# Making a triangular inverse by block rows in the chunk preparation of a gated DeltaNet layer

## The chip, the cores and the metric

The kernel runs on one core of a Trainium2 chip. A core has five engines with queues of their own: TensorE (PE in the profile, with its weight loads as PEld), VectorE (DVE), ScalarE (ACT), GpSimd (POOL) and SyncE (SP), which here only issues DMAs. Each engine works through its queue in order. Matrix products land in PSUM, and DVE or ACT bring them into SBUF. The metric is the device time of one execution in microseconds (us), as the median of several runs.

## The reference

One layer of a diffusion backbone: a gated DeltaNet scan (group A, 4 heads of 128), neighbourhood attention (group B), an output projection and a feed-forward part. Only the preparation of group A matters here. Per chunk of tokens, head and scan direction, the reference solves with a unit triangular matrix:

```python
m = jnp.where(strict, jnp.einsum("bhncd,bhnmd->bhncm", kb, k) * decay, 0.0)
a_mat = jnp.eye(CHUNK, dtype=f32) + m
u = lax.linalg.triangular_solve(a_mat, v * beta[..., None], left_side=True, lower=True, unit_diagonal=True)
w = lax.linalg.triangular_solve(a_mat, kb * jnp.exp(gam)[..., None], left_side=True, lower=True, unit_diagonal=True)
...
v_new = u_i - jnp.einsum("bhck,bhkv->bhcv", w_i, S)
```

There are 1024 latent and 256 context tokens, scanned forward and backward from the context's final state.

## The kernel before

The kernel works on 1280 tokens, features by tokens, in stages: modulation and norm (up to about 60 us), the input projection in blocks of 128 columns (to about 610 us), then the scan beside the attention (to about 850 us), the output projection, and the feed-forward part. Chunks of the scan are 128 tokens here, so there are 10 chunks (2 of context) in each of 2 directions, 20 in all, and each has 4 heads.

The input projection runs over a list of jobs. A `Block` job makes 128 columns with 8 steps of 9 (or 6) matrix products (line 389, tile `blk`); a `Wide` job makes 256 or 264 columns for one token tile after the other (line 572). Both use weights and activations split into a high and a low float32r part, so three products stand for one. Between these products the loop at lines 1008 to 1015 (and 994 to 1007) calls `bg.step(n)`, which moves a background generator on by `n` yields. One of these is `preps()` (line 853), which prepares the chunks.

`preps()` keeps up to three `prep` generators alive and gives each one step in turn, so three chunks are interleaved. It starts after `block_inverses()`, which has inverted all 32x32 diagonal blocks and stored them and their transposes in `x_d`. The first four chunks are those of the context; the others start only when the queries' blocks are done. Within one `prep`:

- Two products with the decay mask (`rg`, line 886, on POOL) are prepared. The diagonal blocks are copied from the loaded tile `xc` into zeroed tiles: the transposed ones into `fx` (ACT, line 891), the inverses into `x0` (POOL, line 892).
- Lines 896 and 897 make the decay exponents in PSUM; line 900 takes the exponential into `e` (ACT). Line 902 multiplies the key products `kk` by it, one DVE instruction per head. The diagonal 32x32 blocks of `kk` are zero, and it is strictly triangular in blocks.
- Line 910 multiplies `kk` by the diagonal inverses (4 heads, one product each), and ACT copies the result over `kk`, now called `f` (line 912).
- Three rounds follow (lines 916 to 922). Each makes `f`-transposed times the present estimate for all 4 heads, 128x128 each (line 919), and DVE adds `x0` into `y` (line 920). With four blocks on the diagonal, the third round is exact.
- `y` is stored in `y_d` (line 929, on SP) two steps later, and the scan reads it from there (line 1067).

Tile `y` is the same buffer as `e` (tag `y`, 4 buffers); `x0` has 3 buffers and `fx` 2, all zeroed once by POOL at line 866. A product of float32 operands appears in the trace as two passes, each a weight load (PEld) and a matrix product (PE). The order of instructions on each engine is fixed when the program is built.

Of the kernel before, what the change touches and what calls it, by code (L numbers as in the profile page):

```python
# [14 lines left out]
OP = mybir.AluOpType  # L15
# [72 lines left out]
def hybrid(ctx, tc, a, dbg):  # L88
    nc = tc.nc
    pe, act, dve, pool, sp = nc.tensor, nc.scalar, nc.vector, nc.gpsimd, nc.sync  # L90

    def pools(stack, name, side=None, bufs=1, **kw):
        if side:
            kw["side"] = side
        return stack.enter_context(tc.tile_pool(name=name, bufs=bufs, reuse_waits="tile", **kw))

    def shift(stack, name, side, n):

        pools(stack, name, side).tile([128, n], F32, name=name, tag=name)
# [142 lines left out]
    hs = [slice(h * 128, h * 128 + 128) for h in range(4)]  # L242
# [117 lines left out]
    with ExitStack() as bs:  # L360
# [7 lines left out]
        def bank(name="m"):  # L368

            if len(psum) == 1:  # L370
                return psum[0].tile([128, 512], F32, name=name, tag="ps")
            return psum[1].tile([128, 512], F32, name=name, tag=name, bufs=4 if name == "blk" else 2)
# [229 lines left out]
        with ExitStack() as xs:  # L602
# [67 lines left out]
            for s0, n in SEGS:  # L670
                p = bank()
# [7 lines left out]
            for k in range(KT):  # L679
# [3 lines left out]
                t = xt[k]  # L683
# [165 lines left out]
        fl = lambda x: x.rearrange("p a b -> p (a b)")  # L849
# [3 lines left out]
        def preps():  # L853

            first_half.close()
            with ExitStack() as gs:
                pk = pools(gs, "pk", "left")
                shift(gs, "ppad", "left", 64)
                pp = pools(gs, "pp", "left")

                def work(name, bufs=2, dt=F32):
                    return (pk if name == "kk" else pp).tile([128, 4, 128], dt, name=name, tag=name, bufs=bufs)

                x0s, fxs = [[work(f"{m}{i}", 1) for i in range(k)] for m, k in (("x0", 3), ("fx", 2))]
                for t in x0s + fxs:
                    pool.memset(t, 0.0)

                def fetch(d, c):

                    kk, xc = work("kk", 4), pp.tile([128, 2, 4, 32], F32, name="xc", tag="xc", bufs=3)  # L870
                    sp.dma_start(kk, kk_d[:, c])
                    sp.dma_start(xc, x_d[:, d, :, c * 4:c * 4 + 4])
                    at = None
                    if c >= 2:
                        at = work("at", 3)
                        sp.dma_start(at, qk_d[:, c - 2])
                    return d, c, kk, xc, at

                def prep(n, d, c, kk, xc, at):
                    lat = c >= 2  # L880
                    mle = M[C_LE + d].rearrange("p (o i) -> p o i", o=1).to_broadcast([128, 4, 128])
                    rgs = []
                    for gg in (GH, GL):
                        rg = work("rg", 2, F32R)
                        src = gg.bitcast(F32)[:, d, c].rearrange("p (h o) -> p h o", o=1).to_broadcast([128, 4, 128])
                        pool.tensor_tensor(rg, src, mle, OP.mult)
                        rgs.append(rg)
                    x0, fx = x0s[n % 3], fxs[n % 2]
                    for b in range(4):
                        q = slice(b * 32, b * 32 + 32)  # L890
                        act.copy(fx[q, :, q], xc[q, 1])
                        pool.tensor_copy(x0[q, :, q], xc[q, 0])
                    yield 1
                    p = bank("pr")
                    for j, rg in enumerate(rgs):
                        pe.matmul(p, mr[:, d], fl(rg), start=j == 0, stop=False)
                    pe.matmul(p, mr[:, 4], mneg[:, d].rearrange("p (o i) -> p o i", o=1).to_broadcast([128, 4, 128]),
                              start=False, stop=True)
                    e = work("y", 4)
                    act.activation(fl(e), p, AF.Exp)  # L900
                    for h in range(4):
                        dve.scalar_tensor_tensor(kk[:, h], kk[:, h], NB[:, d, c, h:h + 1], e[:, h],
                                                 op0=OP.mult, op1=OP.mult)
                    if lat:
                        dve.tensor_tensor(at, at, e, OP.mult)
                        stores.append((at_d[d, c - 2], at, tick[0] + 2))
                    yield 1
                    p = bank("pr")
                    for h in range(4):
                        pe.matmul(p[:, hs[h]], kk[:, h], fx[:, h], start=True, stop=True)  # L910
                    f = kk
                    act.copy(fl(f), p)
                    yield 1
                    y = e
                    src = x0
                    for _ in range(3):
                        p = bank("pr")
                        for h in range(4):
                            pe.matmul(p[:, hs[h]], f[:, h], src[:, h], start=True, stop=True)  # L919
                        dve.tensor_tensor(fl(y), p, fl(x0), OP.add)  # L920
                        src = y
                        yield 1
                    stores.append((y_d[d, c], y, tick[0] + 2))

                stores, tick = [], [0]

                def flush(n):
                    while stores and stores[0][2] <= n:
                        sp.dma_start(*stores.pop(0)[:2])

                todo = [(d, ORDER[d][i]) for i in range(NCH) for d in range(2)]
                live, landing = [], []
                n = 0
                while live or todo or landing:
                    if not landing and todo and (todo[0][1] < 2 or all(x in done for x in queries)):
                        landing.append(fetch(*todo.pop(0)))
                    if landing and len(live) < 3:
                        live.append(prep(n, *landing.pop(0)))
                        n += 1
                    if not live:  # L940
                        yield
                    nxt = []
                    for g in live:
                        tick[0] += 1
                        flush(tick[0])
                        if next(g, 0):
                            nxt.append(g)
                        yield
                    live = nxt
                flush(tick[0] + 2)  # L950
# [23 lines left out]
        for n in range(2, len(jobs) + 2):  # L974
            j = jobs[n] if n < len(jobs) else None
            if n == inv:
                bg2.drain()
                bg2s.close()
                early.close()
                psum.append(bs.enter_context(tc.tile_pool(name="psa", bufs=1, space=PSUM)))  # L980
                bg.add(block_inverses())
                bg.add(preps())
# [52 lines left out]
    fl = lambda x: x.rearrange("p a b -> p (a b)")  # L1035
# [185 lines left out]
    class Stream:  # L1221
# [67 lines left out]
        def next(self, n=2):  # L1289

            while len(self.got) < n:
                self.make()
            out = [self.got.pop(0) for _ in range(n)]
            return out
# [21 lines left out]
    with ExitStack() as os_:  # L1316
# [3 lines left out]
        for k in range(4):  # L1320
            raw = wp.tile([128, KT, 132], F32, name="wraw", tag="wraw", bufs=2)[:, :, :128]
            sp.dma_start(raw, na_d[k].rearrange("p (i t) -> p i t", t=128))
            n = nap.tile([128, 2, L], F32R, name=f"na{k}", tag=f"na{k}")
# [18 lines left out]
        for b in range(KT - 2):  # L1342
# [3 lines left out]
            for k in range(KT):  # L1346
                for j, (wi, xi) in enumerate(((0, 0), (0, 1), (1, 0))):
                    for o, s in zip(outs, HV):
                        pe.matmul(o, w[wi][:, k], parts[xi][k][:, s], start=k == 0 and j == 0,  # L1349
                                  stop=k == KT - 1 and j == 2)  # L1350
# [14 lines left out]
        for t, s in enumerate(HV):  # L1365
            outs = [bank(), bank()]
            last.append(outs)
            for k in range(KT):
                for j, (wi, xi) in enumerate(((0, 0), (0, 1), (1, 0))):
                    for o, w in zip(outs, ws):  # L1370
                        pe.matmul(o, w[wi][:, k], parts[xi][k][:, s], start=k == 0 and j == 0,  # L1371
                                  stop=k == KT - 1 and j == 2)
# [9 lines left out]
    with ExitStack() as us:  # L1382
        xc = pools(ctx, "xc", "right")
# [172 lines left out]
    for n, (wn, xn) in enumerate(zip(Stream.DOWN, FACTORS)):  # L1556
        o = chains[n in (1, 3, 5)]
        for p in range(NFB // 2):
# [4 lines left out]
            for j, b in order:  # L1563
                wi, xi = ((0, 0), (0, 1), (1, 0))[j]
                pe.matmul(o[b], w[wi][:, b], F[xn, p][xi], start=n in (0, 1, 5) and p == 0 and j == 0,  # L1565
                          stop=p == NFB // 2 - 1 and j == 2, skip_group_check=True)
# [79 lines left out]
```

## Time and profile before

| What | Value |
|---|---|
| Median of 3 runs | 1607.62 us (1607.45 to 1609.95) |
| The profiled execution's own time | 1608.33 us |
| Its span in the profile | 1606.5 us |
| Mean granted TensorE clock | 0.982 |
| PE busy | 1504.8 us, 94% |
| DVE, ACT, POOL busy | 1037.5, 713.9, 201.2 us |
| Chunk preparation in the trace | about 288 to 331 us (context) and 425 to 585 us (latent) |

A span is what the profile covers, and the 1.83 us between it and the execution's own time lie around it. In rows of groups, "x320" is the number of instructions, and then come the busy time, the mean of one in nanoseconds and the idle time of the engine just before them. In a row of the timeline come the start, the length from the first start to the last end, the engine, the line and the operation, the tile written and those read, and the count of instructions merged in the row. "128\*32 128x512" is a product with a weight tile of 128 rows and 32 columns and a moving operand of 512 columns.

### The profile page before, as it was taken

How to read it: one execution, taken by the hardware profiler on the slowest of the kernel's cores; microseconds unless marked ns; L12 is line 12 of the kernel's file. 1: busy time of each engine (PE TensorE's matmuls, PEld its weight loads, DVE VectorE, ACT ScalarE, POOL GpSimd, SP SyncE). 2: the span in 40 equal slices, each digit the busy share in tenths (PEclk: the TensorE clock that was granted, in tenths of full speed). 3: DMA queues.
4: the chain of work that ended last, by engine and by line, in shares of the span. 5: the costliest groups of instructions: out<-in, count | busy, mean ns of one | idle time of the engine just before them, and what ended most of it. 6: DMA issues, size and time to landing. Idle time of an engine off the chain costs nothing.

```text
span 1606.5 us, 24016 instructions
## 1 busy us (share of the span) xinstructions
PE 1504.8 (94%) x8594; PEld 1265.4 (79%) x8594; DVE 1037.5 (65%) x1934; ACT 713.9 (44%) x1348; POOL 201.2 (13%) x275
## 2 busy tenths in 40 slices
PE   3999899899999998998997999999999999999999
PEld 1689788678888876787785887888888888888887
DVE  5866588445365665677897449865665655679752
ACT  5342452664434316666674147333333333544441
POOL 2053600512243310000000000000000000000000
PEclk9999999999999998999998999999999999999999
DMA  9366133535545348999846811532232333698742
GB/s 371 125 198 204 57 91 139 181 102 164 164 134 185 99 133 252 284 299 284 247 147 201 277 40 40 190 105 99 103 108 101 116 108 112 229 368 298 260 153 85
DMA packets 211529, 275.23 MB, mean 171 GB/s; under 512 B 15953, under 2 KB 119889, under 8 KB 210385
## 3 DMA queue, kind: packets, MB, share of 16 engines
q1 hardware_dynamic: 210544, 273.06, 52.2%
q8 instruction: 68, 1.11, 0.3%
q10 hardware_dynamic: 864, 0.63, 0.1%
q14 instruction: 53, 0.43, 0.1%
HBM read 206.78 MB, written 71.04 MB: 173 GB/s over the span
## 4 chain that ended last, share of the span: by engine, by line
PE 75%; DVE 7%; DMA 7%; ACT 5%; issue 3%; POOL 2%; SPq 1%; ACTq 0%; DVEq 0%; POOLq 0%
PE ps L1218 26%; PE ps L1565 13%; PE blk L389 10%; PE ps L1349 3%; PE blk L572 3%; PE pr L919 3%; PE sc L317 3%; PE sc L307 2%; PE sc L295 2%; PE pr L910 1%; PE ps L1111 1%; DVE tt L824 1%; PE ps L1371 1%; DMA nv_d<-zt 1%; DMA fraw<-w_conv 1%
## 5 line engine op out<-in xcount | busy, mean ns | idle before, releaser
L389 PE MATMUL blk<-hh,whi 128*128 128x512 f32 (+1 forms) x416 | 125.4, 394 | 4.1 <-ACT whi L198 1.6
L1279 ACT CAST uhi<-ws 128x512 fp32r<-128x512 f32 x91 | 54.7, 622 | 151.2 <-PE ps L1218 76.8
L1279 ACT CAST uhi<-wq 128x512 fp32r<-128x512 f32 x101 | 60.6, 621 | 135.9 <-issue 61.3
L389 PE MATMUL blk<-hh,wlo 128*128 128x512 f32 (+1 forms) x416 | 117.8, 377 | 2.3 <-POOL wlo L199 2.3
L389 PE MATMUL blk<-hl,whi 128*128 128x512 f32 (+1 forms) x416 | 115.5, 375 | 0.0
L1280 DVE TENSOR_TENSOR ulo<-wq,uhi 128x512 fp32r<-128x512 f32 x101 | 67.5, 688 | 66.9 <-ACT uhi L1279 36.9
L1218 PE MATMUL ps<-hT,uhi 128*128 128x512 f32 x336 | 104.3, 392 | 3.1 <-ACT hT L1397 3.1
L1218 PE MATMUL ps<-lT,uhi 128*128 128x512 f32 x336 | 103.6, 390 | 0.0
L1218 PE MATMUL ps<-hT,ulo 128*128 128x512 f32 x336 | 103.5, 389 | 0.0
L1218 PE MATMUL ps<-hB,uhi 128*128 128x512 f32 x288 | 89.7, 392 | 0.0
L1218 PE MATMUL ps<-lB,uhi 128*128 128x512 f32 x288 | 89.2, 391 | 0.0
L1218 PE MATMUL ps<-hB,ulo 128*128 128x512 f32 x288 | 88.9, 389 | 0.0
L389 PEld LDWEIGHTS blk<-hh,wlo 128*128 128x128 f32 x416 | 73.1, 191 | 18.3 <-POOL wlo L199 2.9
L389 PEld LDWEIGHTS blk<-hh,whi 128*128 128x128 f32 x416 | 71.6, 195 | 18.9 <-issue 3.2
L1280 DVE TENSOR_TENSOR ulo<-ws,uhi 128x512 fp32r<-128x512 f32 x91 | 60.8, 687 | 37.5 <-ACT uhi L1279 29.2
L389 PEld LDWEIGHTS blk<-hl,whi 128*128 128x128 f32 x416 | 73.4, 192 | 13.6 <-DVE hl L689 0.3
L572 PE MATMUL blk<-zhi,hh 128*128 128x264 f32 (+1 forms) x288 | 83.9, 291 | 0.0
L572 PE MATMUL blk<-zhi,hl 128*128 128x264 f32 (+1 forms) x288 | 82.1, 285 | 0.0
L572 PE MATMUL blk<-zlo,hh 128*128 128x264 f32 (+1 forms) x288 | 81.7, 284 | 0.0
L198 ACT CAST whi<-wraw 128x1024 fp32r<-128x1024 f32 x26 | 27.3, 1049 | 121.0 <-PE blk L389 50.3
L1218 PEld LDWEIGHTS ps<-hT,uhi 128*128 128x128 f32 x336 | 63.1, 189 | 16.4 <-ACT hT L1397 3.5
L1218 PEld LDWEIGHTS ps<-lT,uhi 128*128 128x128 f32 x336 | 63.4, 189 | 13.2
(333 smaller groups left out, 3738.5 us busy)
## 6 DMA issues: line engine op xcount, KB each, us to landing
wq<-w_fo SPq DMA_DIRECT2D x99, 256.0 KB
wq<-w_gu SPq DMA_DIRECT2D x88, 256.0 KB
wad<-wa SPq DMA_DIRECT2D x64, 256.0 KB
bt<-rpb SPq DMA_DIRECT2D x64, 192.0 KB
t_d<-g SPq DMA_DIRECT2D x22, 512.0 KB
fr<-t_d SPq DMA_DIRECT2D x44, 256.0 KB
f_d<-g SPq DMA_DIRECT2D x33, 256.0 KB
fr<-f_d SPq DMA_DIRECT2D x33, 256.0 KB
```

Of the source, the lines that this page charges most:

```text
L198: act.copy(h, r)
L295: pe.matmul(sc[:, u * 640 + n0:u * 640 + n1], q, ks[i], start=i == 0, stop=i == 1)
L307: pe.transpose(sc[:, u * 640 + j * 128:u * 640 + (j + 1) * 128], bt[:, j * 128:(j + 1) * 128], ident)
L317: pe.matmul(sc[u * ND:u * ND + ND, 1280:1408], vv, pt[:, j * 128:(j + 1) * 128], start=j == 0, stop=j == 4)
L389: pe.matmul(o, ww[:, k], xx[k][:, s], start=k == 0 and j == 0, stop=k == KT - 1 and j == end)
L572: pe.matmul(p[:, :c1 - c0], x[k][:, s], ww[:, k, c0:c1], start=k == 0 and j == 0, stop=k == KT - 1 and j == 2)
L919: pe.matmul(p[:, hs[h]], f[:, h], src[:, h], start=True, stop=True)
L1218: pe.matmul(o, w[wi][:, k], x[xi][:, k], start=first and k == 0 and j == 0, stop=k == n - 1 and j == 2, skip_group_check=True)
L1279: act.copy(hi, self.raw[key])
L1280: dve.tensor_tensor(lo, self.raw[key], hi.bitcast(F32), OP.subtract)
L1349: pe.matmul(o, w[wi][:, k], parts[xi][k][:, s], start=k == 0 and j == 0, stop=k == KT - 1 and j == 2)
L1565: pe.matmul(o[b], w[wi][:, b], F[xn, p][xi], start=n in (0, 1, 5) and p == 0 and j == 0, stop=p == NFB // 2 - 1 and j == 2, skip_group_che ...
```

## The change

The three rounds no longer remake the whole matrix. Each makes one block row of 32 rows, and only the columns that are known by then: 32 columns in the first round, 64 in the second, 96 in the third. The weights of a product are 32 columns of `f`, the output lies on 32 partitions of PSUM, and DVE copies it into these rows of `y` instead of adding `x0`. The diagonal blocks are copied into `y` itself, and so `y` has six zeroed tiles of its own (`x0` had three), and `e` has its own tag with two buffers. The product at line 910 and the ACT copy behind it handle 96 columns of each head instead of 128. The rows that a reused `y` still holds from an earlier chunk meet zeros of `f`.

```diff
-                x0s, fxs = [[work(f"{m}{i}", 1) for i in range(k)] for m, k in (("x0", 3), ("fx", 2))]
-                for t in x0s + fxs:
+                ys, fxs = [[work(f"{m}{i}", 1) for i in range(k)] for m, k in (("y", 6), ("fx", 2))]
+                for t in ys + fxs:
                     pool.memset(t, 0.0)
...
-                    x0, fx = x0s[n % 3], fxs[n % 2]
+                    y, fx = ys[n % 6], fxs[n % 2]
                     for b in range(4):
                         q = slice(b * 32, b * 32 + 32)
                         act.copy(fx[q, :, q], xc[q, 1])
-                        pool.tensor_copy(x0[q, :, q], xc[q, 0])
+                        pool.tensor_copy(y[q, :, q], xc[q, 0])
...
-                    e = work("y", 4)
+                    e = work("e", 2)
...
                     p = bank("pr")
+                    s = slice(32, 128) if d else slice(0, 96)
                     for h in range(4):
-                        pe.matmul(p[:, hs[h]], kk[:, h], fx[:, h], start=True, stop=True)
+                        pe.matmul(p[:, h * 128:h * 128 + 96], kk[:, h], fx[:, h, s], start=True, stop=True)
                     f = kk
-                    act.copy(fl(f), p)
+                    act.copy(f[:, :, s], p.rearrange("p (h i) -> p h i", h=4)[:, :, :96])
                     yield 1
-                    y = e
-                    src = x0
-                    for _ in range(3):
+                    for r in range(1, 4):
                         p = bank("pr")
+                        m, s = (r, slice(0, 32 * r)) if d else (3 - r, slice(128 - 32 * r, 128))
+                        q = slice(32 * m, 32 * m + 32)
                         for h in range(4):
-                            pe.matmul(p[:, hs[h]], f[:, h], src[:, h], start=True, stop=True)
-                        dve.tensor_tensor(fl(y), p, fl(x0), OP.add)
-                        src = y
+                            pe.matmul(p[q, h * 128:h * 128 + 32 * r], f[:, h, q], y[:, h, s], start=True, stop=True)
+                        dve.tensor_copy(y[q, :, s], p[q].rearrange("p (h i) -> p h i", h=4)[:, :, :32 * r])
                         yield 1
                     stores.append((y_d[d, c], y, tick[0] + 2))
```

## The prediction, made before the changed kernel was run

> **What bounds the kernel now.** The page comes first: which engine is full, and what the chain of work that ended last consists of.
>
> ```profile
> span 1606.5 us, 24016 instructions
> PE 1504.8 (94%) x8594; PEld 1265.4 (79%) x8594; DVE 1037.5 (65%) x1934; ACT 713.9 (44%) x1348; POOL 201.2 (13%) x275
> PE 75%; DVE 7%; DMA 7%; ACT 5%; issue 3%; POOL 2%; SPq 1%; ACTq 0%; DVEq 0%; POOLq 0%
> ```
>
> PE is the bound over most of the span, so a microsecond taken from PE moves the end, unless PE then waits. But a share is an average, and the view of windows shows the stages in which the preparation runs.
>
> ```profile
> core 0: us, PE busy (x) PEld busy (x) DVE busy (x) ACT busy (x) POOL busy (x), PEclk, DMA share, GB/s
> 287.00:331.00 44.00, 36.35 (x207) 29.12 (x207) 21.65 (x33) 30.10 (x53) 22.56 (x41) 1.00 0.48 150
> 425.00:586.00 161.00, 149.01 (x998) 134.13 (x997) 100.94 (x160) 63.81 (x125) 62.02 (x92) 0.97 0.43 138
> ```
>
> PE is busy 36.4 of 44 us and 149 of 161 us, at a clock of 1.00 and 0.97. Then the rounds' own line:
>
> ```profile
> L919 PE MATMUL pr<-y,kk x320: 270/275/421, 307.8 to 583.1; 128*128 128x128 f32 x160
> L919 PE MATMUL pr<-x,kk x160: 272/275/421, 302.9 to 574.6; 128*128 128x128 f32 x160
>   DVE y L920: 7.4, 7
> ```
>
> There are 480 passes: 20 chunks, 3 rounds, 4 heads, 2 passes each. The last row says that PE stood idle ahead of this line, waiting for DVE's additions, 7 times for 7.4 us in all. The 275 ns of one is no price, because passes overlap. The price is the pace in the timeline of PE:
>
> ```profile
> 450.35 0.74 PE L389 MATMUL blk<-hh,wlo 128*128 128x256 f32 x3
> 450.93 1.05 PE L919 MATMUL pr<-y,kk 128*128 128x128 f32 x8
> 451.74 0.83 PE L389 MATMUL blk<-hh,whi 128*128 128x256 f32 x3
> ...
> 146.72 0.95 PE L218 MATMUL m<-ones,acc 128*128 128x1 f32 x8
> ...
> L218 PE MATMUL m<-ones,acc x32: 169/250/250, 116.8 to 154.5; 128*128 128x1 f32 x32
> ```
>
> Eight passes last 1.05 us, one alone 0.275: (1.05 - 0.275)/7 = **0.111 us a pass**, 0.89 a round, 53.3 us for 60 rounds. L218, with full weights and one moving column (250 ns alone), keeps (0.95 - 0.25)/7 = 0.100. So the full weight load paces such passes, and cutting columns alone would bring almost nothing. Narrowing the weights to 32 columns is what may.
>
> **PE, part one: the small passes.** The nearest rows are those of L644, which has 32-column weights on a 32-column strip as the new rounds do, and of the float16 products at L295.
>
> ```profile
> L644 PE MATMUL pm<-wada,wide x64: 592/592/617, 27.3 to 51.9; 128*32 128x512 f32 x64
> ...
> 44.88 0.40 PE L389 MATMUL blk<-hl,whi 128*128 128x512 f32 x1
> 45.21 0.12 PEld L644 LDWEIGHTS pm<-wada,wide 128*32 128x32 f32 x3 [0.36 <-issue]
> 45.21 0.62 PE L644 MATMUL pm<-wada,wide 128*32 128x512 f32 x2
> ...
> 46.11 1.02 PE L644 MATMUL pm<-wada,wide 128*32 128x512 f32 x5
> 47.06 0.39 PE L389 MATMUL blk<-hh,whi 128*128 128x256 f32 x1
> 47.06 0.30 PEld L389 LDWEIGHTS blk<-hh,whi 128*128 128x128 f32 x2 [0.84 <-issue]
> ...
> 700.87 0.22 PE L295 MATMUL sc<-kh,qs 128*128 128x128 f16 x1
> 700.92 0.22 PE L295 MATMUL sc<-kl,qs 128*128 128x128 f16 x1
> ...
> 540.03 0.28 PE L389 MATMUL blk<-hl,whi 128*128 128x256 f32 x1
> 597.44 0.62 PE L389 MATMUL blk<-hh,whi 128*128 128x512 f32 x2
> ```
>
> In the row of 46.11, the first belongs to one group of four strips and the last to the next. One alone lasts 0.592 by L644's own row, so the last starts at 46.11 + 1.02 - 0.59 = 46.54, and 512 float32 columns stream in 0.43 us: 0.027 for 32, 0.054 for 64, 0.081 for 96. For a floor of issue, L295 shows a weight load and a product every 0.05 us. I take 0.055 for rounds one and two, the nearer row, and 0.081 for round three. A chunk then costs 8 x (0.055 + 0.055 + 0.081) = 1.53 us instead of 2.67, which **saves 1.14 a chunk and 22.7 us in all**. The bounds are 0.027 in round one (4.5 us more saved) and L218's 0.100 everywhere, where only 480 x 0.011 = 5.3 us are saved. The Trainium skill, in "TensorE: Matmul & The Clock Gate", section "Wait — 56ns, not 53.3ns?", gives the sequencer about 62 ns for a product with hardware decode off; 8 x (0.062 + 0.062 + 0.081) would save 20.6 instead of 22.7. L295's 0.05 is already below that, so the row decides.
>
> **PE, part two: the change of shape.** The same rows show what lies between full products and strips. The last full product starts at 44.88, its 512 columns stream for 0.23 (two such products last 0.62 in the row of 597.44, one 0.40), and so the stream ends at 45.11. The strip's load starts at 45.21, 0.10 later, not ahead of that end; its first product is 0.62 long instead of 0.59, another 0.03. Going back, the strips stream until 46.54 + 0.43 = 46.97, the full load starts at 47.06, and the first full product is 0.39 long, 0.11 more than the 0.28 of 256 columns at 540.03. That is 0.13 in and 0.20 out: **0.33 us a round trip**. At 450.93 and 451.74 no such gap stands now. In PE's timeline the 60 rounds stand in 38 unbroken runs, of one to five rounds; the first and the last are
>
> ```profile
> 302.93 1.06 PE L919 MATMUL pr<-x,kk 128*128 128x128 f32 x8
> ...
> 581.57 1.88 PE L919 MATMUL pr<-y,kk 128*128 128x128 f32 x8
> ```
>
> If the order stays, **38 x 0.33 = 12.5 us are paid back**. If all rounds stood apart it were 60 x 0.33 = 19.8. The Trainium skill speaks against this change on this point: "TensorEngine Tiling (Array Packing)", section "Key Properties", says that changing the tiling mode, not just the tile, drains the engine. The trace agrees, with the 0.33 us above, so the sum by rule and by row is the same.
>
> L910 loses a quarter of its columns but keeps its full weights, and by L218 saves 0 to 0.011 a pass, 1.8 us at most; I take 0. **PE's net: 22.7 - 12.5 = 10.2 us.**
>
> **DVE and ACT.** DVE's addition becomes a copy of 128, 256 and 384 elements on 32 partitions.
>
> ```profile
> L920 DVE TENSOR_TENSOR y<-pr,x 128x512 f32<-128x512 f32 x60 | 41.0, 688 | 39.0 <-PE pr L919 38.5
> L647 DVE COPY arow<-pm 128x512 f32<-128x512 f32 x1 | 0.7, 691 | 6.3 <-PE pm L644 6.3
> L472 DVE COPY SQ<-m 128x8 f32<-128x8 f32 x4 | 0.7, 174 | 27.9 <-PE m L470 27.9
> L912 ACT COPY kk<-pr 128x512 f32<-128x512 f32 x20 | 11.7, 583 | 34.6 <-PE pr L910 34.4
> 578.52 1.16 PE L919 MATMUL pr<-y,kk 128*128 128x128 f32 x8 [2.71 <-DVE y L920]
> ```
>
> A copy out of PSUM costs 0.691 us for 512 elements and 0.174 for 8, about 1.03 ns an element: 0.30, 0.43 and 0.56, or 0.43 on average against 0.688. DVE saves 60 x 0.26 = 15.5 us, but mostly beside PE, since it waits for PE (39.0). On the path lie the 7 waits, 7 x 0.26 = 1.8 us. ACT's copy at 583 ns loses a quarter of its elements, at most 0.15 us, 20 times beside PE's `blk` products, and I count 0. Against the 1.8 stands what PE gains only to wait: the row of 578.52 waits 2.71 us for DVE, which then is in the convolution's work, and a quicker PE waits longer there. I let the two cancel; the bounds are 1.8 either way.
>
> **POOL, SP and space.** No DMA is added or moved, and `y_d` is stored by SP at the same step.
>
> ```profile
> POOL x L892 <- DVE y L920: 43.6, 12, 7.0
> POOL rg L886 <- PE pr L896: 32.5, 10, 8.2
> ...
> L866 POOL MEMSET x<- x3: 530/534/538, 287.9 to 288.9; 128x512 f32 x3
> 297.42 0.61 POOL L892 COPY x<-xc 32x128 f32<-32x128 f32 x2 [5.08 <-DMA xc<-x_d]
> 576.14 1.06 POOL L263 MEMSET bt<- 128x256 f32 x4
> 614.12 0.82 DVE L297 CUSTOM_DVE_ANT_0 bt<-sc,bt 128x640 f32<-128x640 f32 x1 [3.68 <-PE sc L295]
> ```
>
> Six tiles instead of three take away POOL's wait of 43.6 us for the last addition, but behind it POOL still waits for the two `rg` buffers, and no PE row above waits for POOL. I count 0. Three more memsets are 3 x 0.53 = 1.6 us of POOL, hidden by the 5.08 us in which it then waits for `xc`; without that cover they cost 1.6. The larger pool reaches under the first attention tiles, whose memsets stand at 576.14. If these now wait for the last store of `y`, a little after the last round (581.57 + 1.88 = 583.5), they are still over 25 us ahead of the first use at 614.12. No instruction gets a wait that it did not have.
>
> **The sum.** The profiled execution's own time is 1608.33 us, 1.83 of it outside the span. 1608.33 - 10.2 = 1598.1; from the median of the runs, 1607.62, **1597.4 us**. With round one at 0.035 (3.2 more) or both rounds at 0.065 (3.2 less), and the 1.8 either way, this case spans 1592.4 to 1602.4.
>
> **Rivals.**
> - *Shorter still.* Round one at 0.027 (4.5 more), DVE's 1.8 and nothing lost: 17 us saved, 1590.5. For it: the strip loads of L644 start far closer together than 0.055. Against: no row shows a run of loads and products below 0.05.
> - *The rounds come apart.* Where the program's order puts `blk` products between rounds that now adjoin, 60 trips leave 22.7 - 19.8 = 2.9 us: 1604.7, no change that can be told.
> - *The chain takes over.* Inside the longer runs a chunk's next round needs its own copy from DVE. If all runs of more than one round, which hold 33 rounds, gain nothing, the 27 lone ones gain 27 x (0.89 - 0.51 - 0.33) = 1.3: 1606.3. Against: three chunks in turn are 1.53 us of PE, while a round's 0.44, some 0.22 of tail (0.275 - 0.055) and a 0.43 copy are 1.09.
> - *Slower: the trips outweigh the passes.* If a pass, small as it is, still costs the 0.100 of L218, then 12.5 - 5.3 = 7.2 us are lost: 1614.8. It decides from a mean pass of 0.111 - 12.5/480 = 0.085 us. Against: L644's and L295's rows; for: no row shows small float32 passes one behind the other on one strip. The skill's rule on draining, cited above, is part of this case.
> - *It does not do what it says.* If narrow weights were loaded as full ones, the pace would stay at 0.111. The form 128\*32 in L644 excludes it.
>
> **How the numbers follow.** Forecast 0.58, shorter still 0.07, apart 0.10, chain 0.10, slower 0.15. A measurement of this kernel can tell some 0.2% (3.2 us) from no change, so faster is 0.58 + 0.07 = 0.65, the same 0.10 + 0.10 = 0.20, slower 0.15. The range leaves out most of the slower case and the far half of the shortest: 1589 to 1610.
>
> **What would show it.** Eight passes of L919 should last about 0.4 us in rounds one and two and 0.65 in three, between their first and last starts; a gap of about 0.1 ahead of each run's first load and 0.2 behind its last product should stand in PE's timeline, in about 38 places; DVE's copies should take 0.30, 0.43 and 0.56; POOL's wait for DVE should be gone. If a pass stays above 0.085, or PE's waits for DVE between 425 and 586 us grow by as much as the passes shrink, the forecast is wrong.

## The result, and the profile after

| What | Before | After |
|---|---|---|
| Median | 1607.62 us (1607.05 to 1609.95, 5 runs) | 1595.58 us (1594.63 to 1603.28, 5 runs) |
| Ratio of the times | | 0.9932, 95% interval 0.9908 to 0.9956 |
| The profiled execution's own time | 1608.33 us | 1596.21 us |
| Its span | 1606.5 us | 1594.4 us |
| Mean granted TensorE clock | 0.982 | 0.979 |

The kernel became 12.0 us faster; 10.2 were forecast. The page after:

```profile
span 1594.4 us, 23945 instructions
PE 1489.2 (93%) x8594; PEld 1239.2 (78%) x8594; DVE 1019.4 (64%) x1934; ACT 711.0 (45%) x1348; POOL 206.2 (13%) x278
PE 74%; DVE 7%; DMA 7%; ACT 6%; issue 3%; POOL 2%; SPq 1%; ACTq 0%; DVEq 0%; POOLq 0%
```

PE executes as many products as before (8594) and is busy 15.6 us less; DVE is busy 18.1 us less. The chain that ended last has nearly the same make-up. This points at PE, so the gain is looked for in the stage of the preparation. The view of windows, after, for the same two stretches as before:

```profile
core 0: us, PE busy (x) PEld busy (x) DVE busy (x) ACT busy (x) POOL busy (x), PEclk, DMA share, GB/s
287.00:331.00 44.00, 36.05 (x197) 26.02 (x197) 18.30 (x31) 30.75 (x53) 26.62 (x48) 0.96 0.45 145
425.00:586.00 161.00, 151.44 (x1096) 124.83 (x1095) 96.45 (x173) 65.36 (x128) 65.15 (x84) 0.98 0.51 158
```

PE is no emptier in the second stretch than before, but it starts 1096 products there instead of 998. In the same 161 us it gets further, which is what a gain on the bounding engine looks like.

The rounds' own line after (it is now L920, and DVE's copy behind it L921):

```profile
L920 PEld LDWEIGHTS pr<-y,kk x480: 106/110/159, 306.0 to 569.6; 128*32 128x32 f32 x160
L920 PE MATMUL pr<-y,kk x480: 193/219/271, 306.0 to 569.6; 128*32 128x96 f32 x58, 128*32 128x64 f32 x54, 128*32 128x32 f32 x48
  DVE y L921: 1.7, 5
```

The last of them starts at 569.6; before it was 583.1. The weights are loaded as 128\*32, and PE waits 1.7 us for DVE instead of 7.4. PE's timeline shows the three shapes, and what stands around one of them:

```profile
305.95 0.44 PE L920 MATMUL pr<-y,kk 128*32 128x32 f32 x8
311.00 0.63 PE L920 MATMUL pr<-y,kk 128*32 128x64 f32 x8
...
566.70 0.73 PE L389 MATMUL blk<-hl,whi 128*128 128x256 f32 x3
567.27 0.28 PE L389 MATMUL blk<-hh,wlo 128*128 128x256 f32 x1
567.48 0.63 PE L920 MATMUL pr<-y,kk 128*32 128x64 f32 x8
568.04 0.72 PE L389 MATMUL blk<-hh,wlo 128*128 128x512 f32 x2
...
569.04 0.85 PE L920 MATMUL pr<-y,kk 128*32 128x96 f32 x8
```

A round of eight lasts 0.44, 0.63 and 0.85 us where it lasted 1.05. With one product's length taken off (0.20, 0.22 and 0.25, the medians of the three shapes in the trace) seven steps are left of 0.034, 0.059 and 0.086 us. The rounds stand in 52 unbroken runs; 305.95 is the first and 569.04 the last.

Around 567.48 the change of shape can be read. The `blk` product of 567.27 streams its 256 columns in 0.12 (the median distance in this stage from such a product to the next; with 512 columns it is 0.23), so its stream ends at 567.39. The round starts 0.09 later. Its last product starts at 567.48 + 0.63 - 0.22 = 567.89, and the next `blk` product 0.15 later, where 0.06 would be the round's own pace. That product and the next last 0.72 together instead of 0.23 + 0.39 = 0.62. The weight loads at the same place, in the view of PEld:

```profile
567.04 0.19 PEld L389 LDWEIGHTS blk<-hh,wlo 128*128 128x128 f32 x1
567.48 0.47 PEld L920 LDWEIGHTS pr<-y,kk 128*32 128x32 f32 x8 [0.25 <-issue]
568.04 0.30 PEld L389 LDWEIGHTS blk<-hh,wlo 128*128 128x128 f32 x2
```

The load for the `blk` product of 567.27 starts 0.23 ahead of it. The loads for the first product of the round, at 567.48, and for the first one behind it, at 568.04, start only when their products do.

For the whole stage I took the start times of all PE products between the same two `blk` products of both traces (number 1100, ahead of the preparation, and the last one), and gave each distance to the line of the earlier product, up to 0.45 us; the rest counts as waiting.

| us | before | after | difference |
|---|---|---|---|
| the rounds (L919, L920) | 56.4 | 32.1 | -24.3 |
| `blk` products (L389 and L572) | 191.6 | 200.4 | +8.8 |
| the product at L910, now L911 | 19.4 | 18.1 | -1.3 |
| waiting | 19.4 | 17.1 | -2.3 |
| the whole stage | 324.4 | 305.4 | -19.0 |

The other products of the stage take the same time in both. So 24.3 us left the rounds, and 8.8 came back on the `blk` products: 5.3 on those beside a round, which now stand next to another shape, and 3.9 on those in stretches at half clock (a granted clock of 0.5), which cost 5.6 us more than the pace here and 1.7 before; the rest cost 0.4 less. Of the 19.0, 2.4 had been lost ahead of the stage, which starts between 283.5 and 286.7 us in the profiles compared below, and 4.5 are lost behind it, which leaves the 12.1 of the spans.

### The profile page after: what moved, and what is told of

It is laid out like the page before. It is cut to its first block, busy times and chain, and to the rows that moved or that the text cites. A ratio compares the mean times of both kernels' runs of the same rounds, so it can differ in the third digit from the quotient of the medians.

```text
span 1594.4 us, 23945 instructions
## 1 busy us (share of the span) xinstructions
PE 1489.2 (93%) x8594; PEld 1239.2 (78%) x8594; DVE 1019.4 (64%) x1934; ACT 711.0 (45%) x1348; POOL 206.2 (13%) x278
## 4 chain that ended last, share of the span: by engine, by line
PE 74%; DVE 7%; DMA 7%; ACT 6%; issue 3%; POOL 2%; SPq 1%; ACTq 0%; DVEq 0%; POOLq 0%
PE ps L1218 26%; PE ps L1565 13%; PE blk L389 11%; PE blk L572 4%; PE ps L1349 4%; PE sc L317 2%; PE pr L920 2%; PE sc L307 2%; PE sc L295 1%; PE ps L1111 1%; DVE tt L824 1%; PE ps L1371 1%; DMA fraw<-w_conv 1%; PE pr L911 1%; PE ps L1128 1%
## 5 line engine op out<-in xcount | busy, mean ns | idle before, releaser
L389 PE MATMUL blk<-hh,whi 128*128 128x512 f32 (+1 forms) x416 | 127.3, 399 | 4.1 <-ACT whi L198 1.6
L389 PE MATMUL blk<-hh,wlo 128*128 128x512 f32 (+1 forms) x416 | 120.8, 385 | 2.3 <-POOL wlo L199 2.3
L389 PE MATMUL blk<-hl,whi 128*128 128x512 f32 (+1 forms) x416 | 119.2, 380 | 0.0
L389 PEld LDWEIGHTS blk<-hh,wlo 128*128 128x128 f32 x416 | 75.3, 197 | 19.2 <-POOL wlo L199 2.9
L389 PEld LDWEIGHTS blk<-hh,whi 128*128 128x128 f32 x416 | 72.2, 197 | 20.3 <-issue 3.0
L572 PE MATMUL blk<-zhi,hh 128*128 128x264 f32 (+1 forms) x288 | 85.2, 296 | 0.4 <-ACT kk L534 0.4
L389 PEld LDWEIGHTS blk<-hl,whi 128*128 128x128 f32 x416 | 74.4, 194 | 14.1
L572 PE MATMUL blk<-zhi,hl 128*128 128x264 f32 (+1 forms) x288 | 83.4, 290 | 0.0
L572 PE MATMUL blk<-zlo,hh 128*128 128x264 f32 (+1 forms) x288 | 82.7, 287 | 0.0
L1218 PEld LDWEIGHTS ps<-hT,ulo 128*128 128x128 f32 x336 | 63.4, 189 | 13.2
```

Of the source, the lines that this page charges most:

```text
L389: pe.matmul(o, ww[:, k], xx[k][:, s], start=k == 0 and j == 0, stop=k == KT - 1 and j == end)
L572: pe.matmul(p[:, :c1 - c0], x[k][:, s], ww[:, k, c0:c1], start=k == 0 and j == 0, stop=k == KT - 1 and j == 2)
L1218: pe.matmul(o, w[wi][:, k], x[xi][:, k], start=first and k == 0 and j == 0, stop=k == n - 1 and j == 2, skip_group_check=True)
```

## The experiments

Three theories were open, and within the first of them the price of a trip, which is a change from one shape to the other and back.

- **P**: PE's small passes are the gain, less a price for each trip between the shapes.
- **D**: DVE's shorter copies are the gain.
- **O**: POOL's wait or the buffers are the gain.
- Within P, whether a trip costs 0.33 us (**T**) or much less (its rival).

Each run is compared with the kernel before, on the same chip. The rounds compute the same in all of them, some with more rows or columns than are used. Medians are in us.

| Run | Median | Kernel before | Ratio and interval |
|---|---|---|---|
| full weights | 1611.55 | 1608.56 | 1.0015 (1.0001 to 1.0028) |
| full products | 1607.75 | (shared) | 0.9999 (0.9986 to 1.0011) |
| four tiles `x0` | 1608.9 | (shared) | 1.0001 (0.9989 to 1.0012) |
| long copies | 1595.27 | (shared) | 0.9914 (0.9899 to 0.9929) |
| a trip in the middle | 1618.88 | 1607.97 | 1.0075 (1.0059 to 1.0091) |
| the same product at the end | 1611.18 | (shared) | 1.0013 (1.0001 to 1.0025) |
| four strips | 1594.45 | 1607.97 | 0.9914 (0.9898 to 0.9930) |
| third round full | 1594.99 | (shared) | 0.9916 (0.9898 to 0.9934) |
| alternating | 1746.52 | 1606.71 | 1.0844 (1.0776 to 1.0913) |
| grouped | 1691.64 | 1606.71 | 1.0539 (1.0504 to 1.0575) |

### Full weights, short columns

The changed kernel with all 128 columns of `f` as weights; the copy reads the same 32 rows.

```diff
-  pe.matmul(p[q, h * 128:h * 128 + 32 * r], f[:, h, q], y[:, h, s], start=True, stop=True)
+  pe.matmul(p[:, h * 128:h * 128 + 32 * r], f[:, h], y[:, h, s], start=True, stop=True)
```

> The three rounds keep their new columns (32, 64, 96) and their short copies, but each product takes all 128 columns of f as weights, so no strips and no change of shape are left. Theory P (TensorE: the small passes pay, the trips take part of it back): passes at 0.100 to 0.111 us save 0 to 5.3 us, and a little comes from DVE, so 1600 to 1606 us. Theory D (VectorE: the copies of a quarter, a half and three quarters of the length are the gain, since TensorE waits less): as fast as the changed kernel or faster, 1591 to 1597 us. Theory O (POOL and buffers: the wait for the last addition is gone): as D.

1611.55, no gain at all. P had put it at 1600 to 1606, so even the little that short columns were to save is missing; D and O had put it at 1591 to 1597. The row of the rounds' line in this kernel:

```profile
L920 PEld LDWEIGHTS pr<-y,kk x480: 186/192/338, 305.9 to 591.2; 128*128 128x128 f32 x160
L920 PE MATMUL pr<-y,kk x480: 190/276/453, 305.9 to 591.3; 128*128 128x64 f32 x60, 128*128 128x96 f32 x52, 128*128 128x32 f32 x48
```

The moving operand is as short as in the changed kernel, but a load takes 0.192 us instead of 0.110, and the median distance from one start to the next is 0.112, as before the change. Cutting columns alone brings nothing; with full weights the pace stays where it was. The kernel is even 3 us slower, just beyond the noise; the stage of its profile has a granted clock of 0.95, that of the kernel before 0.98, and whether the edit lowers it is open.

### Full weights, full columns

The same with full products, so that only the copies, the tiles and L911 differ from the kernel before.

```diff
-  pe.matmul(p[q, h * 128:h * 128 + 32 * r], f[:, h, q], y[:, h, s], start=True, stop=True)
+  pe.matmul(p[:, hs[h]], f[:, h], y[:, h], start=True, stop=True)
-  dve.tensor_copy(y[q, :, s], p[q].rearrange("p (h i) -> p h i", h=4)[:, :, :32 * r])
+  dve.tensor_copy(y[q, :, s], p[q].rearrange("p (h i) -> p h i", h=4)[:, :, s])
```

> As the run before, and the products also run over all 128 columns of y, so that TensorE's rounds are those of the kernel before the change, 0.89 us each, and only the copies, the tiles and line 911 are new. Theory P: 1604 to 1608 us, no gain. Theory D: 1593 to 1599 us. Theory O: as D.

1607.75, no different from the kernel before. The shorter copies, the six tiles and the shorter product at L911 are all in it, and together they are worth nothing that can be told.

### One tile more for `x0`

The kernel before with four tiles `x0` in place of three.

```diff
-  x0s, fxs = [[work(f"{m}{i}", 1) for i in range(k)] for m, k in (("x0", 3), ("fx", 2))]
+  x0s, fxs = [[work(f"{m}{i}", 1) for i in range(k)] for m, k in (("x0", 4), ("fx", 2))]
-  x0, fx = x0s[n % 3], fxs[n % 2]
+  x0, fx = x0s[n % 4], fxs[n % 2]
```

> The kernel before the change with four x0 tiles instead of three, so that POOL's copy no longer waits for the last addition of the chunk three places earlier. Theory O: most of the gain, 1595 to 1601 us. Theories P and D: no change, 1606 to 1609 us.

1608.9, no difference. But this run doesn't answer what it was made for. What POOL waits for at L892 in this kernel:

```profile
  DVE y L920: 51.1, 14
```

A fourth tile left POOL's wait for DVE standing (52.5 us and 13 times in the same view of the kernel before; the 43.6 of the prediction are those behind 425 us). The answer comes from the run ahead of it. The same wait in the kernel with full products:

```profile
  DMA y_d<-y: 16.1, 2
  PE pr L920: 12.1, 3
```

There, with six tiles, no wait for DVE is left at this line, though POOL still idles for other things, and the time is that of the kernel before. That POOL no longer waits for DVE is worth nothing that can be told.

### Long copies

The changed kernel, with a second DVE copy ahead of each, so that DVE works longer (two copies of 0.28 and 0.41 us at the medians, 0.69 together, as the addition took).

```diff
+  pad = pp.tile([128, 4, 32], F32, name="pad", tag="pad", bufs=1)
...
+  w = (32, 32, 8)[r - 1]
+  pv = p[q].rearrange("p (h i) -> p h i", h=4)
+  dve.tensor_copy(pad[q, :, :w], pv[:, :, :w])
   dve.tensor_copy(y[q, :, s], p[q].rearrange("p (h i) -> p h i", h=4)[:, :, :32 * r])
```

> The changed kernel with a second copy out of PSUM ahead of each copy into y, of 128, 256 and 32 elements, so that a chunk's three rounds cost DVE about 2.1 us again, as before the change, instead of 1.3. Theory P: 0 to 3 us lost against the changed kernel, 1596 to 1599 us. Theory D: most of the gain lost, 1603 to 1608 us. Theory O: 1596 us.

1595.27: the gain is whole. D falls, and O fell with full products. P stands: the gain is the narrow weights'.

### A trip more in each round, and the same product at the end

Two kernels with one small product of full weights and one column in each round, read by nobody: once between the second head and the third, once behind the fourth.

```diff
   for h in range(4):
       pe.matmul(p[q, h * 128:h * 128 + 32 * r], f[:, h, q], y[:, h, s], start=True, stop=True)
+      if h == 1:
+          pe.matmul(p[:, 511:512], ident, ones[:, 0:1], start=True, stop=True)
```

> The changed kernel with one tiny product of full shape (128-column weights, one moving column, into a column of PSUM that nobody reads) between the second and the third head of every round: two passes of about 0.10 us and one more round trip between shapes in each of 60 rounds. Theory T (a round trip costs 0.33 us of TensorE, and this is what takes back most of what the small passes save): 1595.5 + 60 x 0.2 + 60 x 0.33 = 1627 us. Rival (the trip is mostly hidden, about 0.1): 1613 us.

> The control for the run before: the same tiny product behind the fourth head, where a full product mostly follows anyway (52 of 60 rounds in the changed kernel), so that its two passes are paid, but hardly a trip. Theory T: 1595.5 + 12 + 8 x 0.33 = 1607 to 1610 us, 17 to 20 us below the run before. Rival: within 6 us of the run before.

1618.88 and 1611.18: 7.7 us apart, where T said 17 to 20 and its rival at most 6. In the timelines the one kernel has 114 runs of narrow products, the other 62, so 52 more trips cost 0.15 us each, less than half of what T said. PE's timeline of the kernel with the product in the middle, and then of the other, shows a second round in each:

```profile
440.46 0.41 PE L920 MATMUL pr<-y,kk 128*32 128x64 f32 x4
440.80 0.38 PE L922 MATMUL pr<-ones,cst 128*128 128x1 f32 x2
441.11 0.41 PE L920 MATMUL pr<-y,kk 128*32 128x64 f32 x4
441.45 0.61 PE L389 MATMUL blk<-hh,whi 128*128 128x256 f32 x2
```

```profile
443.13 0.63 PE L920 MATMUL pr<-y,kk 128*32 128x64 f32 x8
443.70 0.38 PE L921 MATMUL pr<-ones,cst 128*128 128x1 f32 x2
443.94 0.60 PE L389 MATMUL blk<-hh,whi 128*128 128x256 f32 x2
```

From the round's start to the next `blk` product there are 0.99 and 0.81 us: the trip costs 0.18 here. That is less than the trip to a `blk` product. A likely reason, not tested, is that a product of one column has no stream long enough to hide the next load, with or without a trip, so that there is no hidden load to lose.

### Alternating and grouped

The clean measurement of a trip: eight small products behind each round, four narrow and four full, once in turn and once in two groups. Only the order differs.

```diff
+  for _ in range(4):
+      pe.matmul(p[q, 510:511], ident[:, q], ones[:, 0:1], start=True, stop=True)
+      pe.matmul(p[:, 511:512], ident, ones[:, 0:1], start=True, stop=True)
```

> Behind every round stand four products of one column with 32 columns of weights, in the round's strip, and four of one column with full weights, in turn: narrow, full, narrow, full. Nobody reads them. The other kernel of this pair has the same eight products with the four narrow ones first. Only the order differs, and with it the number of round trips between the two shapes, by 3 a round, 180 in all. Theory (a trip costs 0.33 us wherever TensorE is the bound): this kernel is 180 x 0.33 = 59 us slower than its pair, some 1735 us. Rival (a trip costs about 0.15, as the pair with one small product per round gave): 27 us slower, some 1700 us.

> The same eight products behind every round, the four narrow ones first and then the four with full weights, so that each round has one trip as before. By what one small full product per round cost (16 us for 60 of them, two passes each) the 240 full ones cost 55 to 62 us and the 240 narrow ones about 20: 1670 to 1680 us under both theories; the difference to the pair decides.

1746.52 and 1691.64: 54.9 us for 180 trips, 0.305 each. Both kernels are slower than either theory put them (1735 or 1700, and 1670 to 1680). By the difference T would have it. But PE's timelines, of the alternating kernel and then of the grouped one, say otherwise:

```profile
456.73 0.44 PE L920 MATMUL pr<-y,kk 128*32 128x32 f32 x8
457.00 0.20 PE L922 MATMUL pr<-ones,cst 128*32 128x1 f32 x2
457.13 0.38 PE L923 MATMUL pr<-ones,cst 128*128 128x1 f32 x2
457.45 0.22 PE L922 MATMUL pr<-ones,cst 128*32 128x1 f32 x2
...
458.53 0.38 PE L923 MATMUL pr<-ones,cst 128*128 128x1 f32 x2
458.77 0.59 PE L389 MATMUL blk<-hh,whi 128*128 128x256 f32 x2
```

```profile
445.18 0.44 PE L920 MATMUL pr<-y,kk 128*32 128x32 f32 x8
445.45 0.39 PE L922 MATMUL pr<-ones,cst 128*32 128x1 f32 x8
445.77 1.05 PE L924 MATMUL pr<-ones,cst 128*128 128x1 f32 x8
446.69 0.59 PE L389 MATMUL blk<-hh,whi 128*128 128x256 f32 x2
```

The same work takes 2.04 us and 1.51 us: 0.53 for three trips, 0.18 each, as in the pair before. The other rounds of both kernels that stand ahead of a `blk` product at full clock differ by the same 0.53, and those at half clock by 0.52. 180 x 0.18 = 32 us. What is left of the 54.9 goes with the granted clock. The windows of the alternating kernel and of the grouped one:

```profile
425.00:660.00 235.00, 229.24 (x1567) 208.23 (x1566) 64.49 (x135) 58.00 (x117) 54.27 (x76) 0.77 0.30 96
```

```profile
425.00:660.00 235.00, 229.25 (x1818) 205.91 (x1819) 86.04 (x170) 65.42 (x129) 62.30 (x84) 0.83 0.32 100
```

0.77 against 0.83, where the changed kernel has 0.98 between 425 and 586 us. Over the whole stage it is 0.82 for 460.7 us and 0.88 for 403.6, so some 83 and 48 us of clock were not granted. The difference can cover the 23 us that are left, if the work goes with the clock, which is not shown. So a trip between small products costs 0.18 at full clock. Whether it is the alternation that lowers the clock further, these two profiles can't say.

### Four heads in four strips

Each head's new rows go to another strip of 32 partitions, so that the four may stream side by side. The copies are then four, two on DVE and two on ACT.

```diff
   for h in range(4):
-      pe.matmul(p[q, h * 128:h * 128 + 32 * r], f[:, h, q], y[:, h, s], start=True, stop=True)
-  dve.tensor_copy(y[q, :, s], p[q].rearrange("p (h i) -> p h i", h=4)[:, :, :32 * r])
+      pe.matmul(p[32 * h:32 * h + 32, 0:32 * r], f[:, h, q], y[:, h, s], start=True, stop=True)
+  for h in range(4):
+      (dve.tensor_copy if h < 2 else act.copy)(y[q, h, s], p[32 * h:32 * h + 32, 0:32 * r])
```

> The changed kernel with the four heads of a round on four strips (head h writes partitions 32h to 32h+31), so that their passes run side by side as at line 644, and four copies of one head each bring the rows to their place, two on DVE and two on ACT. Theory T: passes fall from 1.44 to about 0.36 us a chunk, the trips stay, so up to 21 us less: 1575 to 1585 us. Rival (the copies, twice as many per engine and in the way of the next round, become the bound): 1593 to 1605 us.

1594.45: as the changed kernel, in the rival's range. The passes did become cheaper: by the same account the rounds take 19.9 us of PE instead of 32.1. Part of the 12.2 us went into waiting. What PE waits for ahead of the rounds in this kernel:

```profile
  ACT y L922: 12.3, 25
  ACT kk L913: 6.6, 12
  ACT e L900: 4.5, 6
```

A copy on ACT stands behind ACT's other work, and 25 times a round waits for it. These waits stand in place of others, so all waiting in the stage is 21.2 instead of 17.1, 4.1 more. The order fixed at the build has 68 runs of narrow products instead of 52, and the `blk` products take 206.0 us instead of 200.4. The rest lies on the other products. The stage is 306.0 us long, against 305.4.

### The third round with full weights

The third round's pass gains least, so here it has full weights and needs no trip.

```diff
-  pe.matmul(p[q, h * 128:h * 128 + 32 * r], f[:, h, q], y[:, h, s], start=True, stop=True)
+  o, g = (p, f[:, h]) if r == 3 else (p[q], f[:, h, q])
+  pe.matmul(o[:, h * 128:h * 128 + 32 * r], g, y[:, h, s], start=True, stop=True)
```

> The changed kernel with full 128-column weights in the third round alone, where a lone narrow round costs 0.69 + 0.33 = 1.02 us and a full one 0.89. Theory T: 1592 to 1596 us, a gain of 0 to 3 us over the changed kernel. Theory that narrow passes alone pay, and trips hardly: 8 x 0.025 x 20 = 4 us lost, 1599 us.

1594.99: as the changed kernel, within T's range; the 1599 of the other theory lies outside the interval. There are 37 runs of narrow products instead of 52, the rounds take 36.7 us instead of 32.1, waiting is 14.7 instead of 17.1, and the stage takes 305.1. Fifteen trips fewer pay for slower passes. By the pace a third round alone gains 8 x (0.112 - 0.086) = 0.21 us, somewhat less than a trip, so this edit was bound to be worth little, and none of the runs beats the changed kernel by more than the intervals.

## Why the prediction was right, by its steps

**PE bounds the stage, and narrow weights are what counts.** Shown: with full weights the gain is gone, with or without short columns.

**The small passes.** The forecast was 0.055, 0.055 and 0.081 us a pass. Measured were 0.034, 0.059 and 0.086. Round one was mis-sized: L295's 0.05, taken as a floor of issue, is none for such passes. (The Trainium skill's 62 ns for a product, which the prediction named from "TensorE: Matmul & The Clock Gate", section "Wait — 56ns, not 53.3ns?", isn't one here either.) The first step of a run is some 0.02 longer than the others; with the quartiles and the median of all distances between two starts (0.032, 0.056, 0.082) a chunk costs 8 x 0.170 = 1.36 us instead of the 1.53 forecast, 3.4 us less in all.

**What the rounds cost before.** This was the largest miss, and it was not in the new kernel. The 53.3 us of the forecast are 480 clean passes. In the trace of before, 47 of 441 distances within the rounds were over 0.15 us, and these cost 4.4 us more than the pace. PE's timeline of before shows some of them:

```profile
562.78 1.95 PE L919 MATMUL pr<-y,kk 128*128 128x128 f32 x16
564.61 1.16 PE L919 MATMUL pr<-x,kk 128*128 128x128 f32 x8
565.61 2.16 PE L919 MATMUL pr<-y,kk 128*128 128x128 f32 x16
```

Sixteen passes should last 0.275 + 15 x 0.111 = 1.94, and the first row does; the others are late by 0.11 and 0.22. 18 of the 47 lie in three stretches at half clock, and the other 29 at the border of a round (22 are its first step, 7 the step to the next round). In the changed kernel none of 427 such distances is over 0.15.

**The trips.** The price was about right and the number was wrong. Around 567.48 a trip costs 0.09 in, 0.09 and 0.10 out, together 0.28, and by the medians over the stage 0.10, 0.09 and 0.11, together 0.30, where the same places cost 0.01 before; 0.33 was forecast. A cost at a change of mode, which fits the drain that the Trainium skill states without a price ("TensorEngine Tiling (Array Packing)", section "Key Properties"), is seen here at that size. But there are 52, not 38: with shorter rounds the order fixed at the build puts `blk` products between more of them. The rival of the rounds coming apart came true for more than half of the way, at 52 x 0.30 = 15.6 us instead of 12.5.

**The sum of these.** The account has -24.3 + 8.8 = -15.5 for the rounds and the `blk` products. By where the distances lie, this is -26.6 for the pace of the passes (the forecast's -22.7, 3.4 for the shorter passes, and 0.112 for 0.111 before), -4.6 for what before lost within its rounds, +12.1 at the ends of the runs and on the `blk` products beside them, +3.9 for `blk` products at half clock, and -0.4 for the rest. The 12.1 are 14.1 after less 2.0 that the same places cost before, and part of the 15.6 falls on other products. So the forecast's 12.5 for the trips came out by luck: more of them, but less for each in the difference of the two traces. Two terms the forecast did not have, what before lost and the half clock, nearly cancel.

**L910, DVE, ACT, POOL.** L911 gained 1.3 us on PE (0 taken, bound 1.8). DVE's copies lie at 0.28, 0.42 and 0.55 (the medians of the three lengths), close to the 0.30, 0.43 and 0.56 forecast, and lengthening them costs nothing. POOL's wait for DVE went, and what took its place at L892 is a wait for the store of `y`; PE waits for none of it. The rows after for L921 and L892:

```profile
L921 DVE COPY y<-pr x60: 273/420/565, 306.5 to 569.9; 32x128 f32<-32x128 f32 x20, 32x256 f32<-32x256 f32 x20, 32x384 f32<-32x384 f32 x20
```

```profile
  DMA y_d<-y: 12.1, 3
```

**The chain doesn't take over.** PE's waits between 425 and 586 us, after:

```profile
PE pr L911 <- DVE kk L902: 5.7, 5, 3.8
PE pr L911 <- issue: 3.1, 2, 2.8
PE pr L896 <- ACT kk L913: 0.7, 1, 0.7
```

None of these is for a round's own copy. The largest is for DVE's products at L902, ahead of the rounds.

**From the stage to the end.** The prediction let the stage's gain pass to the end unchanged. It did not: 19.0 us in the stage became 12.1. To see what of this is chance, the kernels with narrow weights (the changed one, long copies, four strips, third round full) stand against those with full weights (before, full weights, full products, four tiles), each by one profile:

| us | full weights | narrow weights | difference of means |
|---|---|---|---|
| stage of the preparation | 320.8 to 328.2 | 305.1 to 306.4 | -18.1 |
| from the last `blk` product to the feed-forward part | 365.5 to 370.7 | 369.9 to 372.5 | +2.9 |
| feed-forward part | 625.1 to 626.6 | 626.4 to 627.9 | +1.0 |

Some 4 us of 18 come back behind the stage. One place on the chain of the changed kernel, in order of time:

```profile
776.51 0.16 POOL bt L263
776.67 3.17 DMA bt<-rpb
```

A load of the attention's bias tiles ends last there, and the DMA engines are nearly full in that part, as the window shows (its next to last figure). They were as full before, 0.95 between 700 and 800 us.

```profile
683.00:783.00 100.00, 91.08 (x847) 79.22 (x845) 79.02 (x287) 63.78 (x177) 8.76 (x27) 0.98 0.94 275
```

Whether this is what gives the 4 us back is not shown. The ranges behind the stage overlap, so with eight profiles even the size of the loss stays open. The forecast of 1597.4 came within 1.8 us of the time, and this was in part luck: a gain that was too small (10.2 for the rounds, by the account 15.5) met losses ahead of the stage and behind it that the forecast did not have. The mechanism, cheaper passes less a price for each trip, is what the runs show.

Of the prediction's rivals, "shorter still" adds up to 4.5 + 1.8 + 10.2 = 16.5 us, which is 1591.1 and not 1590.5. It was half right: round one did go below 0.05, but with DVE's copies made long again nothing of the gain is lost.

## What to carry to other kernels

Small float32 products with few moving columns kept the pace of their full weights here, so cut the weight columns and not only the moving ones. Price each boundary between the shapes, not each product, count the boundaries in the order that the new kernel will have, and don't take the old code at its clean pace. A microsecond saved on the bounding engine in one stage is not yet one at the end: compare several profiles stage by stage.

## What the runs showed of the hardware that was not expected

- Narrow float32 passes on one strip follow each other at 0.032 us with 32 columns, weight load included, though the load alone takes 0.110 and the product 0.19: so loads and products overlap several deep. In four strips the median distance is 0.007 us.
- Changing between 128\*32 and 128\*128 costs 0.18 us a round trip between small products and 0.30 beside `blk` products, whose next load is then not made ahead.
- The alternating and the grouped kernel ran at a granted clock of 0.77 and 0.83 between 425 and 660 us, where the changed kernel has 0.98 between 425 and 586. The cause is open.
